# Weight parts issued behind the last eviction, and query weights behind the scores' low part

## The chip, the cores and the metric

One core of a Trainium2 chip runs one launch of the kernel. The metric is the device time of a launch in microseconds (us); a kernel is run three times and the median counts. The engines are named as in the profile: PE (TensorE), ACT (ScalarE), DVE (VectorE), POOL (GpSimd) and SP (SyncE, which here only starts transfers).

## The reference, cut to what matters

An encoder layer is applied to two requests, a prompt of 1024 tokens (A) and a sample of 512 (B), with the same weights. All numbers are 32-bit floats.

```python
h = rms_norm(x, pre_w)
cols = jnp.einsum('bsd,dc->bsc', h, w_in)
m_qk, m_v, m_o, m_z, m_i, m_f, a_qkv, a_z, gate = jnp.split(cols, ..., axis=-1)
y_m = mlstm_mixer(m_qk, m_v, m_o, m_i, m_f, ...) * silu(m_z)
y_a = dilated_attention(a_qkv, rel_table) * silu(a_z)
p_m = jnp.einsum('bsc,cd->bsd', y_m, w_pm)
p_a = jnp.einsum('bsc,cd->bsd', y_a, w_pa)
g = sigmoid(gate).reshape(b_, s_, 2, D_MODEL)
out = jnp.einsum('bsd,de->bse', g[:, :, 0] * p_m + g[:, :, 1] * p_a, w_out)
return x + rms_norm(out, post_w)
```

`mlstm_mixer` is a scan in chunks of 128 positions, in both directions, for four heads of 256 channels. In each chunk the scores q·k are weighted by an exponential of the gates (sc), num = sc·v + (wa·q)·C, and the state C is updated by C = decay·C + (ws·k)ᵀ·v. `dilated_attention` is a softmax over a window of keys, for three strides.

## The kernel before

A product of 32-bit floats is made of three matmuls (`mm3`, L209 to L211): each operand is split into a high part and a low part, and PE adds high·high, high·low and low·high. So everything that PE multiplies is first split: ACT copies the high part, and DVE or POOL subtracts it to get the low one.

*Order of work.* The prompt's projections fill the first 966 us. Then come the prompt's scan (64 rounds: 4 heads, 8 chunks, 2 directions; about 997 to 1310 us), the prompt's attention (to about 1635), the sample's scan (32 rounds; to about 1833), the sample's attention (to about 1957), and the merging of the branches with the last product. From 966 us on, "dense" units stand between the steps of scans and attention: products of 128 columns of a weight matrix with 512 tokens, for the sample's projections and later the branches. Each unit collects in one of two PSUM banks and is then emptied by an *eviction*: a function of its own for each kind of unit (`silu`, L746 and L749; `att_unit`, L772 and L774; the convolution's raw copy, L870; the gate's tanh, L896; `proj_m` and `proj_a`, L1643 and L1660; `close`, L1704 to L1711). PE can begin a unit only when the one before the last has been evicted.

*Weights.* `load_w` brings 512 KB into one of two raw buffers (`wraw`), by SP or, from the prompt's attention on, by POOL's queue. `split_w` (L263 to L283) issues the high part on ACT (L272) and the low part on DVE (L278) into a ring of pairs (`wh`/`wl`, later also `X0` and `Q1`). A raw buffer is free for the next load when the low part is done.

*Who sets the order.* PE's order and, from 966 us on, SP's are written by hand. Each other engine has one queue, worked off in order, whose order a scheduler picks at build time from its own estimates; `issue_after(x)` makes it put an instruction behind x. `split_w` already puts both parts behind `self.held` (the last four attention instructions on ACT or DVE), and the low part also behind `self.scans` (the scan's last DVE results).

*The scan.* `front(k)` prepares round k: POOL selects a mask (rm, L1103), ACT takes the exponential (L1105), DVE multiplies by the scores (L1106), ACT copies the high part (sch, L1109), POOL subtracts the low one (scl, L1110). From the second chunk on POOL also weights the queries with a row tile rw that a transfer brings (qw, L1114), ACT copies their high part (L1117), POOL subtracts the low one (ql, L1118). `core(k)` makes the products `num` and `kv` and updates the state: cf (L1149 for the first chunk, L1152 later), then its parts ch (L1176) and cl (L1177). There is one buffer for `kv`, so the next `kv` waits for cf.

*The attention.* For each tile of 128 queries: `products` (PE, lg), `softmax` (DVE adds the bias and takes the row maximum, L1374; nm, L1376; ACT takes exponentials, L1378), `turn` (PE transposes, L1385; a copy pts on ACT, L1388, or DVE, L1390) and `output` (PE o, L1398; ACT ot, L1400). The merged mLSTM rows ymr are split beside it (K0 on ACT, L1594; K1 on DVE, L1595).

Of the kernel before, what the change touches and what calls it, by code (L numbers as in the profile page):

```python
# [22 lines left out]
F32 = mybir.dt.float32  # L23
F32R = mybir.dt.float32r
AF = mybir.ActivationFunctionType
OP = mybir.AluOpType
# [3 lines left out]
P = 128  # L30
D = 1024
KT = D // P
BLK = 512
# [148 lines left out]
class Net:  # L182
    def __init__(self, tc, a):
        self.tc, self.nc, self.a = tc, tc.nc, a
        self.clock = self.lag = 0
        self.pending, self.owner = [], {}
        self.defer, self.mixed, self.rows = False, set(), {}
        self.queued, self.pace = [], 1
        self.side = self.nc.sync
        self.lows = None  # L190
        self.scans, self.state, self.held, self.sum = [], [], [], None
        self.low_part = None
        self.retired = []
        self.narrow, self.acc, self.direct = {}, [None, None], {}

# [68 lines left out]
    def split_w(self, raw, n):  # L264

        nc = self.nc
        hi, lo = self.wsplit.pop(0)
        self.wsplit.append((hi, lo))
        with ExitStack() as st:
            for x in self.held:  # L270
                st.enter_context(self.tc.issue_after(x.ins))
            high = nc.scalar.activation(hi[:, :n], raw[:, :n], AF.Copy)  # L272

        def rest():
            with ExitStack() as st:
                for x in (*self.held, *self.scans):
                    st.enter_context(self.tc.issue_after(x.ins))
                low = (self.lows or nc.vector).tensor_sub(lo[:, :n], raw[:, :n], hi[:, :n].bitcast(F32))  # L278
# [463 lines left out]
    def silu(self, c, g, w):  # L742

        nc = self.nc
        th = w()
        nc.scalar.activation(th, c, AF.Tanh, scale=0.5)  # L746
        if g is None:
            g = th
            nc.vector.scalar_tensor_tensor(g, th, 1.0, c, op0=OP.add, op1=OP.mult)  # L749
        else:  # L750
            nc.vector.scalar_tensor_tensor(g, th, 1.0, g, op0=OP.add, op1=OP.mult)
        return g
# [7 lines left out]
    def att_unit(self, j, c, T, w):  # L760

        nc, S = self.nc, T.S
        keys, g = j >= 12, j % 12 // 4
        dil = min(DILS[g], S // P)
        hi, lo = w(F32R), w(F32R)
        if g == 0 and not keys:
            parts = [(hi[:, :S - 64], lo[:, :S - 64], c[:, 64:]), (hi[:, S - 64:], lo[:, S - 64:], c[:, :64])]
        else:
            by = lambda z: z.rearrange("p (r i) -> p r i", r=dil)
            parts = [(by(hi), by(lo), c.rearrange("p (i r) -> p r i", r=dil))]  # L770
        for h, _, x in parts:
            nc.scalar.activation(h, x, AF.Copy, scale=1.0 if keys else 0.125)  # L772
        for h, l, x in parts:
            nc.vector.scalar_tensor_tensor(l, x, 1.0 if keys else 0.125, h.bitcast(F32), op0=OP.mult, op1=OP.subtract)  # L774
# [87 lines left out]
    def short_units(self, T):  # L862

        nc = self.nc
# [2 lines left out]

        def conv(u):
            def use(p):
                nc.scalar.activation(self.sraw[:, 1:1 + BLK], p, AF.Copy)  # L870
                self.conv_unit(u, T, self.sraw, w, False)
            return self.unit(u, use)

# [19 lines left out]
        def gate(br, ct):  # L893
            def use(p):
                t = w()
                nc.scalar.activation(t, p, AF.Tanh, scale=0.5)  # L896
# [139 lines left out]
    def mlstm(self, T, fill, steps, first, banks, lead, after, beside=()):  # L1036
# [10 lines left out]
        with ExitStack() as stack:  # L1047
# [45 lines left out]
            def front(k):  # L1093
# [13 lines left out]
                sch = sb.tile([P, P], F32R, name="sch")  # L1107
                scl = sb.tile([P, P], F32R, name="scl")
                nc.scalar.activation(sch, rm, AF.Copy)  # L1109
                nc.gpsimd.tensor_sub(scl, rm, sch.bitcast(F32))  # L1110
                m = made[k] = {"rw": rw, "sc": (sch, scl), "fl": flc}
                if i > 0:
                    qw = sb.tile([P, 2, P], F32, name="qw")
                    nc.gpsimd.tensor_tensor(qw, x["q"][:, :, cs], rw[:, 1][:, None, :].to_broadcast([P, 2, P]), op=OP.mult)  # L1114
# [502 lines left out]
    def branches(self, T, b, odd, before):  # L1617
# [12 lines left out]
        def proj_m(weights):  # L1630
            m2[:] = [self.place(1 - odd, i, F32) for i in (0, 2)]
            gate(1, 0)
            for ct in range(KT):
                wm = weights()
                pm = self.dense()
                for k in range(KT):
                    c = slice(k * P, (k + 1) * P)
                    hi, lo = yb[k // 4]
                    self.mm3(pm, (wm[0][:, c], wm[1][:, c]), (hi[:, k % 4], lo[:, k % 4]), k == 0, k == KT - 1)
                    if k == 3:  # L1640
                        gate(*((1, ct + 1) if ct < KT - 1 else (0, 0)))
                    if k == KT - 1:
                        nc.vector.scalar_tensor_tensor(m2[ct // 4][:, ct % 4], gates.pop((1, ct)), 1.0, pm, op0=OP.add, op1=OP.mult)  # L1643
                    yield

        def proj_a(weights):
            for ct in range(KT):
# [5 lines left out]
                for k in range(4):  # L1653
# [3 lines left out]
                        gate(0, ct + 1)  # L1657
                    if k == 3:
                        mg = self.osb.tile([P, BLK], F32, name="mg", bufs=2)
                        nc.vector.scalar_tensor_tensor(mg, gates.pop((0, ct)), 1.0, pa, op0=OP.add, op1=OP.mult)  # L1660
# [21 lines left out]
    def final(self, T, b):  # L1682
# [4 lines left out]
        def make(weights):  # L1687
# [13 lines left out]
            def close(u, t, c, p):  # L1701
                r0 = b * BLK + t * P
                o1 = sb.tile([P, BLK], F32, name="mg", bufs=2) if u else o[t]
                nc.scalar.activation(o1, p, AF.Square, accum_out=ss[:, t, u:u + 1])  # L1704
                if u == 0:
                    nc.vector.tensor_mul(o[t], p, pw[:, c])
# [4 lines left out]
                nc.vector.tensor_mul(o1, p, pw[:, c])  # L1711
# [339 lines left out]
```

## Time and profile before

| what | value |
|---|---|
| runs | 2256.8, 2258.14 and 2259.2 us, median 2258.14 |
| profiled execution | 2261.5 us, of which 1.8 outside the span |
| span, first to last instruction | 2259.7 us |
| busy: PE / DVE / ACT / POOL | 2244.2 / 1509.5 / 1129.2 / 718.6 us |
| granted TensorE clock | 1.000 |
| DMA | 418.27 MB, mean 185 GB/s |

A row of the timeline gives the start (from the span's start), the duration, the engine and line, what is written and read, and in brackets how long the engine had been idle and what ended that. A wait of PE counts in the end only because PE's order is fixed: whatever it waits for moves all that follows. An idle engine beside it costs nothing by itself.

### The profile page before, as it was taken

What the parts mean: (1) busy time and instruction counts of PE and PEld (TensorE: products, weight loads), DVE (VectorE), ACT (ScalarE), POOL (GpSimd) and SP (SyncE); (2) the same over time, 40 slices, a digit from 0 to 9 for tenths busy, and PEclk for the clock granted to TensorE, in tenths of its full rate; (3) what the DMA queues carried; (4) which work ended last, traced back from release to release, by engine and by line L of the source; (5) the groups of instructions that cost most, each with busy time, mean ns of one, the idle gap of its engine ahead of it and who ended that gap; (6) DMA issues with size and microseconds to landing.
All of it is one profiled execution on the core that took longest, in us unless ns stands there. A gap on an engine that the chain in (4) does not pass through costs nothing.

```text
span 2259.7 us, 35388 instructions
## 1 busy us (share of the span) xinstructions
PE 2244.2 (99%) x12226; PEld 1964.6 (87%) x12226; DVE 1509.5 (67%) x2875; ACT 1129.2 (50%) x2369; POOL 718.6 (32%) x1000
## 2 busy tenths in 40 slices
PE   9999999999999999999999999999999999999998
PEld 8999888888888888888888899999888888888887
DVE  7765577687776556558887755544689844655674
ACT  6432244344444434357777655566665644554332
POOL 1000333333333223237676610011165522221221
PEclk9999999999999999999999999999999999999999
DMA  3652455543332223284664789997678797776663
GB/s 123 168 134 76 172 205 192 192 176 121 112 111 103 84 84 140 103 298 153 226 223 127 191 217 235 253 245 221 203 248 284 238 278 211 233 251 200 233 230 109
DMA packets 222685, 418.27 MB, mean 185 GB/s; under 512 B 24841, under 2 KB 128969, under 8 KB 222506
## 3 DMA queue, kind: packets, MB, share of 16 engines
q1 hardware_dynamic: 194536, 315.86, 44.4%
q0 software_dynamic: 24368, 87.56, 12.4%
q10 hardware_dynamic: 3602, 12.59, 1.4%
q8 instruction: 97, 1.59, 0.3%
q14 instruction: 82, 0.67, 0.1%
HBM read 296.19 MB, written 128.12 MB: 188 GB/s over the span
## 4 chain that ended last, share of the span: by engine, by line
PE 95%; DMA 2%; issue 1%; ACT 1%; POOL 1%; DVE 0%; DVEq 0%; SPq 0%; POOLq 0%; ACTq 0%
PE d L211 14%; PE d L209 14%; PE d L210 14%; PE dense L209 12%; PE dense L211 12%; PE dense L210 12%; PE o L1398 4%; PE pt L1385 2%; PE lg L1362 2%; PE num L211 1%; PE num L209 1%; PE num L210 1%; PE kv L209 1%; PE a L1070 1%; PE kv L210 1%
## 5 line engine op out<-in xcount | busy, mean ns | idle before, releaser
L209 PE MATMUL dense<-H,wh 128*128 128x512 f32 x664 | 270.6, 408 | 0.8 <-DVE V0b L1643 0.8
L211 PE MATMUL dense<-H,wl 128*128 128x512 f32 x664 | 260.9, 393 | 0.0
L210 PE MATMUL dense<-H,wh 128*128 128x512 f32 x664 | 260.2, 392 | 0.0
L210 PE MATMUL d<-Hl,phla 128*128 128x512 f32 x608 | 236.5, 389 | 0.0
L211 PE MATMUL d<-Hh,phla 128*128 128x512 f32 x608 | 236.5, 389 | 0.0
L209 PE MATMUL d<-Hh,phla 128*128 128x512 f32 x608 | 236.5, 389 | 0.0
L278 DVE TENSOR_TENSOR wl<-wraw,wh 128x1024 fp32r<-128x1024 f32 (+1 forms) x121 | 149.3, 1234 | 70.0 <-ACT wh L272 69.9
L1374 DVE CUSTOM_DVE_ANT_0 ls<-lg,bias 128x256 f32<-128x256 f32 (+1 forms) x288 | 93.7, 362 | 132.8 <-PE lg L1362 71.2
L211 PE MATMUL d<-Hh,phlb 128*128 128x512 f32 x456 | 177.4, 389 | 0.0
L209 PE MATMUL d<-Hh,phlb 128*128 128x512 f32 x456 | 177.4, 389 | 0.0
L210 PE MATMUL d<-Hl,phlb 128*128 128x512 f32 x456 | 177.4, 389 | 0.0
L687 POOL TENSOR_TENSOR psum_w<-pw_raw 128x512 f32<-128x512 f32 x38 | 58.0, 1527 | 365.1 <-DMA pw_raw<-w_in 208.8
L1378 ACT ACTIVATE ls<-ls,nm 128x256 f32<-128x256 f32 (+1 forms) x288 | 130.3, 454 | 84.0 <-DVE nm L1376 59.2
L272 ACT ACTIVATE wh<-wraw 128x1024 fp32r<-128x1024 f32 (+1 forms) x124 | 128.7, 1038 | 77.1 <-PE dense L210 27.0
L211 PEld LDWEIGHTS dense<-H,wl 128*128 128x128 f32 x664 | 124.6, 188 | 28.2
L209 PE MATMUL d<-vhi,Hh 128*128 128x322 f32 x448 | 140.9, 315 | 0.3
L211 PE MATMUL d<-vhi,Hl 128*128 128x322 f32 x448 | 140.3, 313 | 0.4 <-DVE Hl L396 0.2
L210 PE MATMUL d<-vlo,Hh 128*128 128x322 f32 x448 | 139.7, 312 | 0.0
L209 PEld LDWEIGHTS dense<-H,wh 128*128 128x128 f32 x664 | 125.0, 188 | 15.5 <-DVE V0b L1643 1.2
L210 PEld LDWEIGHTS dense<-H,wh 128*128 128x128 f32 x664 | 125.4, 189 | 14.3
L211 PEld LDWEIGHTS d<-Hh,phla 128*128 128x128 f32 x608 | 114.1, 188 | 23.7
L210 PEld LDWEIGHTS d<-Hl,phla 128*128 128x128 f32 x608 | 114.2, 188 | 23.6
(570 smaller groups left out, 6166.4 us busy)
## 6 DMA issues: line engine op xcount, KB each, us to landing
pw_raw<-w_in SPq DMA_DIRECT2D x76, 512.0 KB
wraw<-w_in SPq DMA_DIRECT2D x64, 512.0 KB
aqk_a<-pwk SPq DMA_DIRECT2D x48, 512.0 KB
aqk_b<-sw SPq DMA_DIRECT2D x48, 256.0 KB
wraw<-w_pm POOLq DMA_DIRECT2D x24, 512.0 KB, 6.1
wraw<-w_out POOLq DMA_DIRECT2D x24, 512.0 KB, 4.0
wraw<-w_v POOLq DMA_DIRECT2D x22, 430.0 KB, 7.3
erep<-erow SPq DMA_DIRECT2D x16, 512.0 KB
```

The lines of the kernel that those rows point to most:

```text
L209: nc.tensor.matmul(out, lh, rh, start=start, stop=False)
L210: nc.tensor.matmul(out, lh, rl, start=False, stop=False)
L211: nc.tensor.matmul(out, ll, rh, start=False, stop=stop)
L272: high = nc.scalar.activation(hi[:, :n], raw[:, :n], AF.Copy)
L278: low = (self.lows or nc.vector).tensor_sub(lo[:, :n], raw[:, :n], hi[:, :n].bitcast(F32))
L687: self.nc.gpsimd.tensor_add(s[:, 0], ws[1][:, 0], ws[1][:, 1])
L1070: nc.tensor.matmul(p[:, c - c0], kT[:, ct, c * P:(c + 1) * P], qT[:, ct, c * P:(c + 1) * P], start=ct == 0, stop=ct == 1)
L1362: nc.tensor.matmul(lg[:, hh, c:c + w], q[hh][:, qs], z[:, k0:k0 + w], start=z is k[hh], stop=z is not k[hh])
L1374: nc.vector.tensor_tensor_reduce(out=ls[:, hh], in0=ts["lg"][hh], in1=bt[:, hh], scale=1.0, scalar=NEG, op0=OP.add, op1=OP.max, accum_out= ...
L1378: self.held = self.held[-3:] + [nc.scalar.activation(ls[:, hh], ls[:, hh], AF.Exp, bias=nm[:, hh:hh + 1], accum_out=ot[:, 128 + hh:129 + hh])]
L1385: nc.tensor.transpose(pp[:, hh * nk + x], ts["ls"][:, hh, x * P:(x + 1) * P], self.ident)
L1398: nc.tensor.matmul(po[:, hh * 64:hh * 64 + 64], pt[:, hh * nk + x], v[:, kt[x], c0 + hh * 64:c0 + hh * 64 + 64], start=x == 0, stop=x == n ...
```

## The change

Two edits. First, each eviction notes its instructions in `self.evicted`, and `split_w` puts the high part and the low part of a weight behind those of the last eviction, besides `self.held`. Second, in the first eight rounds of each scan the weighting of the queries on POOL is put behind the low part of the scores of the same round. Nothing is added or taken away; PE's order and SP's stay as they are.

```diff
         self.scans, self.state, self.held, self.sum = [], [], [], None
-        self.low_part = None
+        self.low_part, self.evicted = None, []
...
         with ExitStack() as st:
-            for x in self.held:
+            for x in (*self.held, *self.evicted):
                 st.enter_context(self.tc.issue_after(x.ins))
             high = nc.scalar.activation(hi[:, :n], raw[:, :n], AF.Copy)
 
         def rest():
             with ExitStack() as st:
-                for x in (*self.held, *self.scans):
+                for x in (*self.held, *self.evicted, *self.scans):
                     st.enter_context(self.tc.issue_after(x.ins))
...
-        nc.scalar.activation(th, c, AF.Tanh, scale=0.5)
+        self.evicted = [nc.scalar.activation(th, c, AF.Tanh, scale=0.5)]
         if g is None:
             g = th
-            nc.vector.scalar_tensor_tensor(g, th, 1.0, c, op0=OP.add, op1=OP.mult)
+            self.evicted.append(nc.vector.scalar_tensor_tensor(g, th, 1.0, c, op0=OP.add, op1=OP.mult))
...
-                nc.scalar.activation(t, p, AF.Tanh, scale=0.5)
+                self.evicted = [nc.scalar.activation(t, p, AF.Tanh, scale=0.5)]
...
                 nc.scalar.activation(sch, rm, AF.Copy)
-                nc.gpsimd.tensor_sub(scl, rm, sch.bitcast(F32))
+                low = nc.gpsimd.tensor_sub(scl, rm, sch.bitcast(F32))
...
-                    nc.gpsimd.tensor_tensor(qw, x["q"][:, :, cs], rw[:, 1][:, None, :].to_broadcast([P, 2, P]), op=OP.mult)
+                    with self.tc.issue_after(low.ins) if k < 8 else ExitStack():
+                        nc.gpsimd.tensor_tensor(qw, x["q"][:, :, cs], rw[:, 1][:, None, :].to_broadcast([P, 2, P]), op=OP.mult)
```

The evictions of `att_unit`, the convolution, `proj_m`, `proj_a` and `close` are noted in the same way. Because of added lines, a line of before from L774 on is one higher in the changed kernel, two from L1114 and three from L1644.

Three places show how rows move. The first is POOL at the start of the prompt's scan (about 982 to 1003 us); rm, scl, qw and ql carry a number for their round, rw0 to rw3 are row tiles. Before:

```order
L1103 AFFINE_SELECT rm_8069<-rw0_7902 128x128
L1114 TENSOR_TENSOR qw_8146<-Q0_7883,rw0_7902 128x256
L1103 AFFINE_SELECT rm_8085<-rw1_7903 128x128
L1114 TENSOR_TENSOR qw_8213<-Q0_7883,rw1_7903 128x256
L1110 TENSOR_TENSOR scl_8076<-rm_8069,sch_8075 128x128
L1103 AFFINE_SELECT rm_8136<-rw0_7902 128x128
L1118 TENSOR_TENSOR ql_8149<-qw_8146,qh_8148 128x256
L1118 TENSOR_TENSOR ql_8216<-qw_8213,qh_8215 128x256
L1114 TENSOR_TENSOR qw_8275<-Q0_7883,rw2_7904 128x256
L1110 TENSOR_TENSOR scl_8092<-rm_8085,sch_8091 128x128
L1110 TENSOR_TENSOR scl_8143<-rm_8136,sch_8142 128x128
L1103 AFFINE_SELECT rm_8203<-rw1_7903 128x128
```

In the changed kernel POOL's rows at the same place are:

```order
L1111 TENSOR_TENSOR scl_8092<-rm_8085,sch_8091 128x128
L1111 TENSOR_TENSOR scl_8143<-rm_8136,sch_8142 128x128
L1116 TENSOR_TENSOR qw_8146<-Q0_7883,rw0_7902 128x256
L1104 AFFINE_SELECT rm_8203<-rw1_7903 128x128
L1104 AFFINE_SELECT rm_8265<-rw2_7904 128x128
L1120 TENSOR_TENSOR ql_8149<-qw_8146,qh_8148 128x256
L1111 TENSOR_TENSOR scl_8210<-rm_8203,sch_8209 128x128
L1116 TENSOR_TENSOR qw_8213<-Q0_7883,rw1_7903 128x256
L1104 AFFINE_SELECT rm_8337<-rw3_7905 128x128
L1120 TENSOR_TENSOR ql_8216<-qw_8213,qh_8215 128x256
L1111 TENSOR_TENSOR scl_8272<-rm_8265,sch_8271 128x128
L1116 TENSOR_TENSOR qw_8275<-Q0_7883,rw2_7904 128x256
```

scl_8092 and scl_8143 now stand ahead of all qw, and qw_8275, which waits for row tile rw2, stands behind them; ql_8216 now stands behind the select of rw3.

The second place is ACT at the start of the sample's attention (about 1839 to 1851 us); sw0 and sw1 are evictions of gate units, wh1 is the high part of a weight. Before:

```order
L272 ACTIVATE Q1_18766<-wraw1_7754 128x1024
L272 ACTIVATE wh1_7757<-wraw0_7753 128x1024
L896 ACTIVATE sw0_7871<-dense_18811 128x512
L1378 ACTIVATE ls_18906,ot1_18786<-ls_18906,nm_18907 128x256 x2
L1594 ACTIVATE K0_18817<-ymr0_18770 128x512
L1378 ACTIVATE ls_18955,ot2_18787<-ls_18955,nm_18956 128x256 x2
L896 ACTIVATE sw1_7872<-dense_18879 128x512
```

In the changed kernel ACT has there:

```order
L272 ACTIVATE Q1_18766<-wraw1_7754 128x1024
L897 ACTIVATE sw0_7871<-dense_18811 128x512
L1380 ACTIVATE ls_18906,ot1_18786<-ls_18906,nm_18907 128x256 x2
L1596 ACTIVATE K0_18817<-ymr0_18770 128x512
L1380 ACTIVATE ls_18955,ot2_18787<-ls_18955,nm_18956 128x256 x2
L272 ACTIVATE wh1_7757<-wraw0_7753 128x1024
L897 ACTIVATE sw1_7872<-dense_18879 128x512
```

wh1 moved from ahead of the eviction sw0 to behind the exponentials of ls_18955, just ahead of the next eviction.

The third place is DVE right behind it (about 1846 to 1863 us); wl1, wl2, wl0 and X0 are low parts of weights, ls the softmax tiles. Before:

```order
L278 TENSOR_TENSOR wl1_7758<-wraw0_7753,wh1_7757 128x1024
...
L1390 COPY pts_18917<-pt_18784 128x512
...
L278 TENSOR_TENSOR wl2_7760<-wraw1_7754,wh2_7759 128x1024
L1374 ISA ls_19001,ot3_18788<-lg_18946,bias1_18796 128x256
...
L1376 TENSOR_SCALAR nm_19002<-ot3_18788 128x2
L278 TENSOR_TENSOR wl0_7756<-wraw0_7753,wh0_7755 128x1024
L1374 ISA ls_19061,ot4_18789<-lg_18996,bias2_18797 128x256
...
L1390 COPY pts_19013<-pt_19008 128x512
L278 TENSOR_TENSOR X0_18765<-wraw1_7754,X0_18765 128x1024
L1376 TENSOR_SCALAR nm_19062<-ot4_18789 128x2
```

In the changed kernel DVE has there:

```order
L1392 COPY pts_18917<-pt_18784 128x512
...
L278 TENSOR_TENSOR wl1_7758<-wraw0_7753,wh1_7757 128x1024
L278 TENSOR_TENSOR wl2_7760<-wraw1_7754,wh2_7759 128x1024
L278 TENSOR_TENSOR wl0_7756<-wraw0_7753,wh0_7755 128x1024
L1376 ISA ls_19001,ot3_18788<-lg_18946,bias1_18796 128x256
...
L1376 ISA ls_19061,ot4_18789<-lg_18996,bias2_18797 128x256
...
L1392 COPY pts_19013<-pt_19008 128x512
L1378 TENSOR_SCALAR nm_19002<-ot3_18788 128x2
L1378 TENSOR_SCALAR nm_19062<-ot4_18789 128x2
L278 TENSOR_TENSOR X0_18765<-wraw1_7754,X0_18765 128x1024
```

The three low parts wl1, wl2 and wl0 now stand together ahead of the reductions of ls_19001, which stood ahead of wl0.

More of the change, by code (lines that the diff above doesn't have):

```diff
@@ L771, in att_unit @@
         for h, _, x in parts:
-            nc.scalar.activation(h, x, AF.Copy, scale=1.0 if keys else 0.125)
+            self.evicted = [nc.scalar.activation(h, x, AF.Copy, scale=1.0 if keys else 0.125)]
         for h, l, x in parts:
-            nc.vector.scalar_tensor_tensor(l, x, 1.0 if keys else 0.125, h.bitcast(F32), op0=OP.mult, op1=OP.subtract)
+            low = nc.vector.scalar_tensor_tensor(l, x, 1.0 if keys else 0.125, h.bitcast(F32), op0=OP.mult, op1=OP.subtract)
+        self.evicted.append(low)
         self.put(("aqk", T.S, j), T.aqk[0, j], hi.bitcast(F32), hi)
@@ L869, in use @@
             def use(p):
-                nc.scalar.activation(self.sraw[:, 1:1 + BLK], p, AF.Copy)
+                self.evicted = [nc.scalar.activation(self.sraw[:, 1:1 + BLK], p, AF.Copy)]
                 self.conv_unit(u, T, self.sraw, w, False)
@@ L1642, in proj_m @@
                     if k == KT - 1:
-                        nc.vector.scalar_tensor_tensor(m2[ct // 4][:, ct % 4], gates.pop((1, ct)), 1.0, pm, op0=OP.add, op1=OP.mult)
+                        self.evicted = [nc.vector.scalar_tensor_tensor(m2[ct // 4][:, ct % 4], gates.pop((1, ct)), 1.0, pm,
+                                                                       op0=OP.add, op1=OP.mult)]
                     yield
```

8 lines of the change are left out of this document (4 added, 4 removed).

## The prediction

> **What bounds the kernel now.** I read the page first, then the list of what each engine waited for, then the timeline around each wait.
>
> ```profile
> span 2259.7 us, 35388 instructions
> ...
> PE 2244.2 (99%) x12226; PEld 1964.6 (87%) x12226; DVE 1509.5 (67%) x2875; ACT 1129.2 (50%) x2369; POOL 718.6 (32%) x1000
> ...
> PE 95%; DMA 2%; issue 1%; ACT 1%; POOL 1%; DVE 0%; DVEq 0%; SPq 0%; POOLq 0%; ACTq 0%
> ```
>
> TensorE (PE) is busy for 2244.2 of 2259.7 us and holds 95% of the chain that ended last. Its order is written out by hand and both programs have the same one. So the change can only take away, or add, moments in which PE waits. The list of PE's waits says how many there are; the columns are the sum, the count and the longest, in us:
>
> ```profile
> PE num L211 <- POOL scl L1110: 1.2, 1, 1.2
> PE kv L209 <- DVE cf L1152: 1.2, 2, 0.6
> ...
> PE dense L209 <- DVE V0b L1643: 0.8, 1, 0.8
> PE dense L209 <- ACT sw L896: 0.7, 1, 0.7
> ...
> PE kv L209 <- DVE r L1163: 0.4, 1, 0.4
> PE o L1398 <- ACT pts L1388: 0.2, 1, 0.2
> PE num L209 <- DVE X L1169: 0.2, 1, 0.2
> ...
> PE kv L209 <- DVE cf L1149: 0.2, 1, 0.2
> ```
>
> These rows, with the left-out ones of the start, are all waits of PE that the profile shows. They sum to 4.9 us and all lie behind 990 us, where the reordering begins. A first matmul behind a wait also runs 0.1 us longer (0.50 for 0.39 us in the fourth place below), about 1 us for the nine. **The ceiling of any gain is 6 us**, 0.26%. A measurement of this kernel can tell about 0.2%, or 4.5 us, from no change.
>
> **The change part by part.** No instruction, transfer or byte is added or removed; only rows of ACT, DVE and POOL change places, all between 974 and 1873 us. So each term is one place where PE waits now, or where a moved row may make it wait.
>
> *First place, the start of the prompt's scan.* Timeline of POOL, ACT and PE; the columns are start, duration, engine, line, names, and in brackets the idle time with what ended it:
>
> ```profile
> 997.10 1.19 POOL L1114 TENSOR_TENSOR qw<-Q,rw 128x256 f32<-128x256 f32 x1 [1.68 <-DMA rw<-rw_a]
> 998.25 0.86 POOL L1110 TENSOR_TENSOR scl<-rm,sch 128x128 fp32r<-128x128 f32 x2
> ...
> 994.92 0.31 ACT L1109 ACTIVATE sch<-rm 128x128 fp32r<-128x128 f32 x1 [0.20 <-DVE rm L1106]
> ...
> 998.76 0.39 PE L211 MATMUL num<-V0a,scl 128*128 128x258 f32 x1 [1.17 <-POOL scl L1110]
> ```
>
> POOL stood in qw, which waited for a row tile to land, and the two scl behind it came at 998.25, though the high parts that they need were there by 995.23 (994.92 + 0.31). In the new order both scl stand ahead of every qw. They can run from 995.2, and PE, which has waited since 997.59 (998.76 less 1.17), finds the first of them done even if it takes the longest time of the row at the end of the next fence, 1.44. **Gain 1.2.** The weighting then comes later: qw and ql of rounds 2 and 3 run between 996 and 1003.5, since one select among them waits for the row tile that ended POOL's idling at 1002.31.
>
> ```profile
> 1002.31 1.40 POOL L1114 TENSOR_TENSOR qw<-Q,rw 128x256 f32<-128x256 f32 x1 [2.69 <-DMA rw<-rw_a]
> ...
> 1005.87 0.28 PE L211 MATMUL num<-ch,ql 128*128 128x258 f32 x1
> ...
> 1011.12 0.28 PE L211 MATMUL num<-ch,ql 128*128 128x258 f32 x1
> ...
> L1110 POOL TENSOR_TENSOR scl<-rm,sch x96: 448/468/1439, 984.7 to 1798.2; 128x128 fp32r<-128x128 f32 x96
> ```
>
> PE uses them at 1005.87 and 1011.12, so 7 us cover the move; its cost is 0. If that cover were gone, each us late would cost one. The same edit in the sample's scan moves rows that no wait of PE names: 0.
>
> The last row gives the least, median and longest time of a scl in ns.
>
> *Second place, the end of the same scan, where DVE has no room.* Timeline of ACT, DVE, POOL and PE:
>
> ```profile
> 1278.52 1.05 ACT L272 ACTIVATE wh<-wraw 128x1024 fp32r<-128x1024 f32 x1
> 1279.48 0.57 ACT L746 ACTIVATE sg<-dense 128x512 f32<-128x512 f32 x1
> ...
> 1280.08 0.69 DVE L749 SCALAR_TENSOR_TENSOR sg<-sg,dense 128x512 f32<-128x512 f32 x1 [0.61 <-ACT sg L746]
> ...
> 1281.08 1.58 DVE L278 TENSOR_TENSOR wl<-wraw,wh 128x1024 fp32r<-128x1024 f32 x1
> ...
> 1287.67 0.74 DVE L1152 SCALAR_TENSOR_TENSOR cf<-cf,rw,kv 128x516 f32<-128x516 f32 x1
> 1288.97 0.69 DVE L751 SCALAR_TENSOR_TENSOR sg<-sw,sg 128x512 f32<-128x512 f32 x1 [0.56 <-ACT sw L746]
> ...
> 1281.56 1.42 POOL L1110 TENSOR_TENSOR scl<-rm,sch 128x128 fp32r<-128x128 f32 x1
> ...
> 1284.34 0.36 PE L209 MATMUL kv<-V1a,kh 128*128 128x258 f32 x1 [0.64 <-DVE cf L1152]
> ...
> 1289.23 0.28 PE L209 MATMUL kv<-V1a,kh 128*128 128x258 f32 x1
> ```
>
> Now the weight's high part runs before the eviction sg, DVE idles 0.61 us for that eviction, and everything behind it up to the state update cf is late. With the eviction first, DVE starts 0.5 us or so sooner and the 0.64 wait at 1284.34 nearly goes. But at 1287.67 the new order puts the second eviction (0.69) ahead of cf, which had 0.82 to spare (1289.23 less 1288.41). Moved behind it, cf ends about 0.7 later, and PE comes about 0.5 sooner: up to 0.5 comes back there. The waits near 1277 and 1295 (0.2 and 0.4) may shrink with DVE's idle time. Bounds: 0 to the 1.2 of the three waits. I take the middle, **gain 0.6**. The wait at 1745 keeps its DVE rows ahead of it and stays.
>
> The weight's subtraction took 1.58 us here, beside a scl of 1.42 on POOL, where its like take 1.22 (fourth place) and the median scl 0.47: each seems to hold up the other. [...]
>
> *Third place, the start of the sample's attention.* ACT and PE:
>
> ```profile
> 1844.84 1.06 ACT L272 ACTIVATE wh<-wraw 128x1024 fp32r<-128x1024 f32 x1 [4.68 <-DMA wraw<-w_pm]
> 1845.80 0.58 ACT L896 ACTIVATE sw<-dense 128x512 f32<-128x512 f32 x1
> ...
> 1846.43 0.50 PE L209 MATMUL dense<-H,X 128*128 128x512 f32 x1 [0.72 <-ACT sw L896]
> ```
>
> A high part that waits 4.68 us for its load holds up the eviction behind it, and PE waits for the bank. The new order has the eviction ahead; its unit ended a whole unit of PE's work earlier, since the two banks take turns, so the wait goes. **Gain 0.7.** What is late next is the weight itself, which now stands behind more rows.
>
> *Fourth place, 14 us later, where the change adds a wait.* The weight part wl0 waits for a load, and in the new order the softmax reductions of ls_19001 (L1374) stand behind it instead of ahead:
>
> ```profile
> 1852.38 0.42 DVE L1374 CUSTOM_DVE_ANT_0 ls<-lg,bias 128x256 f32<-128x256 f32 x1
> ...
> 1853.18 0.17 DVE L1376 TENSOR_SCALAR nm<-ot 128x2 f32<-128x2 f32 x1
> 1853.92 1.22 DVE L278 TENSOR_TENSOR wl<-wraw,wh 128x1024 fp32r<-128x1024 f32 x1 [0.56 <-ACT wh L272]
> ...
> 1855.74 0.69 DVE L1390 COPY pts<-pt 128x512 f32<-128x512 f32 x1
> ...
> 1853.79 0.49 ACT L1378 ACTIVATE ls<-ls,nm 128x256 f32<-128x256 f32 x1
> ...
> 1834.69 0.53 POOL L261 DMA_DIRECT2D wraw<-w_pm  x1 [1.78 <-DVE X L278]
> ...
> 1860.66 0.60 PE L1385 MATMUL pt<-ident,ls 128*128 128x128 f32 x4
> ...
> wraw<-w_pm POOLq DMA_DIRECT2D x24, 512.0 KB, 6.1
> ...
> DMA to landing us min/median/max: 5.3/7.7/10.1
> ```
>
> The last two rows give the time from issue to landing: the page's median of these 24 loads, and least, median and longest of the five that POOL issues from 1834 to 1860. Here the chain, each step with its own row's time. The low part X0 of that buffer moves behind two reductions, a subtraction and a small row (0.42 to 0.7 each now), so the load of 1834.69 goes out at about 1836.2. It lands 10.1 later, as now (1844.84 less 1834.69), at 1846.3; high part (1.06) to 1847.4, low part (1.22) to 1848.6, next load out at 1848.9. With the median of 6.1 this lands at 1855.0; high part to 1856.1, low part to 1857.3. Then two reductions and a small row (0.97 now, from 1852.38 to 1853.35), two reductions and a copy (1.29 now, from the end of wl at 1855.14 to 1856.43): 1859.6. Two exponentials of 0.49 end at 1860.6. PE turns that tile at 1860.66, or 1859.9 once the third place's 0.7 is gone. **Loss 0.8**, by bounds of 0 (a load of 5.3) and 4.8 (one of 10.1). I take 6.1 because this very load is the shortest of the five now and will meet the same transfers, but later.
>
> Sum: 1.2 + 0.6 + 0.7 - 0.8 = 1.7 us less. From the profiled execution's 2261.5 (span and 1.8 around it) that gives 2259.8; this execution lies 3.4 above the median of the runs, 2258.14, so the forecast is **2256.4**.
>
> **The rivals.** *Full gain:* the load at the fourth place takes 5.3, and all of the second place's 1.2 goes: 3.1 less, 2255.0. For it: that load takes 5.3 now; against: DVE's lack of room around 1288. Chance 0.18. *Low parts hold up the softmax (the slower side):* every row of DVE behind wl0 waits with it. It decides from a second load of 7.8 us on: there the wait, 2.5, eats all three gains. At 10.1 it is 4.8, and the sum is 2260.4; a second tile late by the same costs 4.8 more, 2265.2. For it: the 10.1 of the first load. Against: behind 1873 us no row moves, so it can hit two or three tiles only. Chance 0.17, a third of it over 2262.7. *Weighting late or GpSimd blocked at the first place:* by times near the longest of the scl row, or by a late row tile, the 1.2 comes back as a wait for ql or scl: 2257.6. Chance 0.08. *The change does not do what it says* is excluded for the order; the rows moved. Something that no row shows: 0.05, mostly slower.
>
> **How the numbers follow.** My forecast has 0.52. Faster by over 0.2% means under 2253.6, which needs 4.5 of the ceiling's 6: 0.04. Slower by over 0.2%, over 2262.7: 0.06 from the slower rival and 0.04 from the unknown, 0.10. The rest, 0.86, is within. The range goes from 2253.8 (3.1 and the spread of the runs, 1.2 to a side) to 2261.0 (the slower rival with one tile late, and 0.7 of that spread).
>
> **What would show it.** Right: the list of PE's waits loses "num <- scl" and "dense <- sw"; kv waits near 1284 shrink; a wait of pt for ACT's ls of 0 to 2.4 us appears near 1859. Wrong: waits of num for ql near 1006, of kv for cf that grow in count, or several of pt or o between 1855 and 1875.

## The result, and the profile after

The change made the kernel slower: 2265.35 us median (2263.6 to 2267.2), against 2258.45 for the kernel before on the same chip; the ratio is 1.0028, with a 95% interval of 1.0021 to 1.0035. The prediction, 2256.4 in a range to 2261.0, was wrong in size and in sign. The profiled execution of the changed kernel took 2264.7 us (span 2262.6), that of before 2261.5, so the two profiles differ by 3.2 of the 6.9 us: before's lies 3 above its own median.

The page of the changed kernel, in the lines that answer to those of before: PE works 1.0 us longer and holds a point less of the chain, DVE a point or two more.

```profile
span 2262.6 us, 35332 instructions
...
PE 2245.2 (99%) x12226; PEld 1966.9 (87%) x12226; DVE 1505.1 (67%) x2875; ACT 1125.5 (50%) x2369; POOL 718.8 (32%) x1000
...
PE 94%; DMA 2%; DVE 2%; issue 1%; ACT 1%; POOL 0%; DVEq 0%; POOLq 0%; ACTq 0%
```

Its list of PE's waits (sum, count, longest in us):

```profile
PE lg L1364 <- DVE ot L1376: 3.3, 1, 3.3
...
PE dense L209 <- ACT sw L897: 1.9, 1, 1.9
PE pt L1387 <- ACT ls L1380: 0.8, 1, 0.8
...
PE num L209 <- ACT X L1169: 0.7, 1, 0.7
```

All that the prediction named is gone: num for scl, the three between 1277 and 1295 (one of num, two of kv), dense for sw at 1846, dense for V0b at 2026. In their place stand two long ones. Where they lie is best seen on one instruction of each tile, the scores lg of the sample's attention. First the kernel before, then the changed one:

```profile
1832.71 0.64 PE L1362 MATMUL lg<-V0a,Q 128*128 128x256 f32 x4
...
1841.88 0.64 PE L1362 MATMUL lg<-V0a,Q 128*128 128x256 f32 x4
...
1854.16 0.72 PE L1362 MATMUL lg<-V1a,Q 128*128 128x256 f32 x4
1860.10 0.72 PE L1362 MATMUL lg<-V1a,Q 128*128 128x256 f32 x4
1866.06 0.72 PE L1362 MATMUL lg<-V1a,Q 128*128 128x256 f32 x4
```

```profile
1828.19 0.64 PE L1364 MATMUL lg<-V0a,Q 128*128 128x256 f32 x4
...
1839.54 0.64 PE L1364 MATMUL lg<-V0a,Q 128*128 128x256 f32 x4
...
1850.80 0.72 PE L1364 MATMUL lg<-V1a,Q 128*128 128x256 f32 x4
...
1855.93 1.00 PE L1400 MATMUL o<-X,pts 128*128 128x64 f32 x8
1860.24 1.20 PE L1364 MATMUL lg<-V1a,Q 128*128 128x256 f32 x4 [3.31 <-DVE ot L1376]
1862.21 1.18 PE L1387 MATMUL pt<-ident,ls 128*128 128x128 f32 x4 [0.77 <-ACT ls L1380]
...
1869.49 0.73 PE L1364 MATMUL lg<-V1a,Q 128*128 128x256 f32 x4
```

The changed kernel comes to the sample's attention 4.5 us ahead (1832.71 less 1828.19). The wait of dense at 1836 takes that to 2.3, the prediction's third place gives back 1.0 (3.4 ahead at 1850.80), and then it loses 6.8 within two tiles: 18.69 us from 1850.80 to 1869.49, where the kernel before needs 11.90. Two waits, 3.31 and 0.77, make 4.1 of that. The rest is TensorE's clock. Stretches of the changed kernel; the columns are the busy times of PE, its weight loads, DVE, ACT and POOL (with counts), then the granted clock, the share of the DMA and GB/s:

```profile
1858.00:1860.00 2.00, 0.00 (x0) 0.00 (x0) 1.82 (x4) 0.80 (x3) 0.30 (x1) 0.81 0.38 143
1860.00:1862.00 2.00, 1.20 (x4) 0.93 (x4) 1.53 (x9) 0.45 (x2) 0.23 (x1) 0.50 0.85 202
...
1866.00:1868.00 2.00, 2.00 (x10) 1.59 (x10) 1.99 (x3) 2.00 (x8) 1.96 (x5) 0.98 0.84 307
```

From 1859.3 to 1866.1 the clock is 0.50, and the dense matmuls begin 0.43 us apart there, behind it 0.23. PE is busy for 5.09 us of that; by the clock I estimate that half of it, 2.5 us, is lost beside the waits. 4.1 and 2.5 make 6.6 of the 6.8. The two are not independent: lg takes 1.20 us in place of 0.72, and pt behind it, which waits for ACT, would have waited that 0.5 longer at full clock. By itself the clock costs about 2.0, an estimate from these rows.

Why does lg wait? ACT, DVE and POOL of the changed kernel, followed back from it:

```profile
1836.53 1.05 ACT L272 ACTIVATE X<-wraw 128x1024 fp32r<-128x1024 f32 x1
...
1846.14 0.51 ACT L1380 ACTIVATE ls<-ls,nm 128x256 f32<-128x256 f32 x1 [2.12 <-DVE nm L1378]
...
1847.14 1.04 ACT L272 ACTIVATE wh<-wraw 128x1024 fp32r<-128x1024 f32 x1
...
1857.09 1.06 ACT L272 ACTIVATE wh<-wraw 128x1024 fp32r<-128x1024 f32 x1 [5.86 <-DMA wraw<-w_pm]
...
1858.18 1.23 DVE L278 TENSOR_TENSOR wl<-wraw,wh 128x1024 fp32r<-128x1024 f32 x1 [6.17 <-ACT wh L272]
1859.32 0.42 DVE L1376 CUSTOM_DVE_ANT_0 ls<-lg,bias 128x256 f32<-128x256 f32 x1
```

```profile
1835.51 0.63 ACT L1596 ACTIVATE K<-ymr 128x512 fp32r<-128x512 f32 x1 [6.38 <-DMA ymr<-ym_a]
```

```profile
1839.13 0.53 POOL L261 DMA_DIRECT2D wraw<-w_pm  x1 [1.42 <-DVE X L278]
...
1849.74 0.53 POOL L261 DMA_DIRECT2D wraw<-w_pm  x1 [4.16 <-DVE wl L278]
```

In order of time: the split K0 of a row tile (an earlier one than the K0_18817 shown under *The change*, which runs at 1843.39) stands on ACT ahead of the eviction sw3 and of X0's high part, and waits 6.38 us for its load. X0's low part, which frees the raw buffer, is late with it, and the load goes out at 1839.13 in place of the 1836.2 that I had worked out for a later PE. It lands 5.9 us later, at 1845.06, but its high part wh1 stands on ACT behind the exponentials of ls_18955 and begins only at 1847.14. The next load goes out at 1849.74 and lands at 1857.0; the low part wl0 follows at 1858.18, and the reductions of ls_19001 stand behind it until 1859.32, though their scores were made two lg before. The lg of 1860.24 needs the bank that they read.

My theory after this was that the loss is made at the sample's attention, by reductions that queue on DVE behind a low part, with the half clock on top. The rivals were that the loads are too slow in any order, that waits differ from execution to execution, and that PE's own lead makes the wait. Each expectation says what its letters stand for.

### The profile page after: what moved, and what is told of

The parts are those of the page before. It is cut to its first block, busy times and chain, and to the rows that moved or that the text cites. A ratio compares the mean times of both kernels' runs of the same rounds, so it can differ in the third digit from the quotient of the medians.

```text
span 2262.6 us, 35332 instructions
## 1 busy us (share of the span) xinstructions
PE 2245.2 (99%) x12226; PEld 1966.9 (87%) x12226; DVE 1505.1 (67%) x2875; ACT 1125.5 (50%) x2369; POOL 718.8 (32%) x1000
## 3 DMA queue, kind: packets, MB, share of 16 engines
q8 instruction: 97, 1.59, 0.3%
## 4 chain that ended last, share of the span: by engine, by line
PE 94%; DMA 2%; DVE 2%; issue 1%; ACT 1%; POOL 0%; DVEq 0%; POOLq 0%; ACTq 0%
PE d L211 14%; PE d L209 14%; PE d L210 14%; PE dense L209 12%; PE dense L211 12%; PE dense L210 12%; PE o L1400 4%; PE pt L1387 2%; PE lg L1364 2%; PE num L209 1%; PE num L211 1%; PE num L210 1%; PE a L1071 1%; DMA ymr<-ym_a 1%; PE kv L210 1%
```

## The experiments

All times are medians; the kernel before was measured beside each set of runs at 2257.9 to 2258.45.

*Each edit alone.* The first edit alone puts `with ExitStack():` back at qw:

```diff
-                    with self.tc.issue_after(low.ins) if k < 8 else ExitStack():
+                    with ExitStack():
```

> The change without its second edit: only the weights' parts behind the evictions. Theory Q (queue): the loss is made in the sample's attention, where a split of ymr that waits for a load stands ahead of an eviction on ACT, and reductions stand behind a weight part that waits for a load on DVE; these loads, not PE, set when the waits end. So giving the 1.2 us of the first scan's start back only shortens the later waits: 2264 to 2266, PE's wait of lg near 1860 about 2 instead of 3.3 us, and the half clock behind it stays. Theory L (late start): the two edits add up independently: 1.3 us slower than the change, 2266.7, with the wait of lg unchanged at 3.3.

Measured: 2266.43, ratio 1.0031 (1.0020 to 1.0043). The whole loss comes from this edit. Its profile has the wait of lg (2.6, shorter, as Q has it), that of pt (1.3) and slow matmuls behind them (the dense ones begin 0.43 us apart, later 0.23), but the time is nearer L's 2266.7; it doesn't tell the two theories apart.

The second edit alone takes `self.evicted` out of both lists of `split_w`:

```diff
-            for x in (*self.held, *self.evicted):
+            for x in self.held:
...
-                for x in (*self.held, *self.evicted, *self.scans):
+                for x in (*self.held, *self.scans):
```

> Only the second edit: query weights behind the scores' low part. Theory Q: PE's wait of num for scl at 998 goes and nothing replaces it in the sample's attention, since its order is that of before: 1 to 1.3 us less than before, 2257.2. Theory E (any earlier PE runs into the transfers of the sample's attention and gives the time back there): same as before within 0.3 us, 2258.4, with a longer wait of dense for sw near 1845.

Measured: 2257.15, ratio 0.9992 (0.9984 to 1.0001): 1.2 us less, as expected and the size of the prediction's first place, though the interval reaches no change. Of the three waits between 1277 and 1295 its profile has one left (0.39).

*Evictions noted for part of the time.* A flag `note` switches the first edit on and off; each kernel sets it at other places:

```diff
-            for x in (*self.held, *self.evicted):
+            for x in (*self.held, *(self.evicted if self.note else ())):
...
-                for x in (*self.held, *self.evicted, *self.scans):
+                for x in (*self.held, *(self.evicted if self.note else ()), *self.scans):
```

Off from the sample's attention on:

> Both edits, but the parts go behind evictions only until the sample's attention begins; there the reductions stand ahead of wl0 again, and X0's high part ahead of the ymr split, while the eviction sw3 still stands behind that split. Theory Q: no wait of lg near 1860 and no half clock; a wait of dense for sw of 1 to 2 us near 1836 and one of 0.7 near 1843 stay: 4.4 earlier up to there, so 2256 to 2257. Theory E: the 4.4 us come back as waits in the sample's attention: 2258 or more.

Measured: 2259.8, ratio 1.0004 (0.9996 to 1.0013). lg doesn't wait, the clock stays at 1.00, and 5.5 us of the loss are gone; but the time is E's and not Q's. Off from the sample's scan on:

> Both edits, but the parts go behind evictions only until the sample's scan begins; from there on the order is that of before. Theory Q: 3 us gained up to 1640 us, all else as before (waits of kv near 1745 and 1777, of dense near 1846): 2255.5. Theory E: 2258 or more, the 3 us coming back as longer waits behind 1830.

Measured: 2258.54, ratio 0.9997 (0.9988 to 1.0006). Again E's side: the parts ahead don't bring the 3 us that the profiles seemed to promise. On only from the middle of the prompt's scan (`k == 31`) to the end of the prompt's attention:

> Both edits, but the evictions are noted only from the middle of the prompt's scan (round 32 of 64) to the end of the prompt's attention: without the new waits near 1078 and 1096 us, and without the sample's scan and attention. Theory Q (the change is worth what its gains at the end of the scan and in the prompt's attention are, 1.3 for the weighting and 1.5 to 2.5 for the evictions): 2258.4 - 1.3 - 2.0 = 2255.1. Rival V (the waits of the kernel before at 1277 to 1295 and 1475 differ from execution to execution and were only long in its profile, so the evictions are worth nothing there): 2257.1, the same as the weighting alone.

Measured: 2255.57, ratio 0.9988 (0.9979 to 0.9997), the fastest kernel of all, and the only one whose interval lies wholly below 1. Q's side; but what the evictions add to the weighting alone, some 1.3, isn't clear of the noise, since the two intervals overlap. PE doesn't wait between 1270 and 1300 in its profile. On only up to the middle of the prompt's scan:

> Both edits, but evictions noted only up to the middle of the prompt's scan (round 32 of 64). Theory Q (the early half costs what the run with late notes lacks against the run with notes up to the sample's scan, 2258.5 - 2255.6 = 3.0): 2257.15 + 3.0 = 2260.1, with waits near 1078, 1082 and 1096 us that the weighting alone doesn't have. Rival V (these two runs differ for other reasons, the waits there are 0.7 us each at most): 2257.2 to 2258.

Measured: 2258.55, ratio 1.0003 (0.9994 to 1.0011), 1.4 more than the weighting alone, between the two expectations. The first half of that scan costs something: in its profile num waits 0.69 for ACT's X at 1096 and kv 0.39 for cf at 1077. The 3.0 between the two runs before it isn't explained by this alone.

*The second profile of the kernel before.*

> The kernel before, once more, for a second profile. Theory V (its short waits for loads and for ACT and DVE behind them differ from execution to execution): the wait of 1.2 for scl at 998 is there again, since it comes from the order on POOL; the waits at 1277 to 1295, 1745, 1846 and 2026 are there in part, with other lengths, and the profiled time lies within 2256 to 2262. Rival F: the same list of waits within 0.1 us each.

```profile
PE num L211 <- POOL scl L1110: 0.9, 1, 0.9
...
PE kv L209 <- DVE cf L1152: 0.6, 1, 0.6
...
PE dense L209 <- ACT sw L896: 0.2, 1, 0.2
```

2259.21 us. Theory V holds: scl is there again (0.9 for 1.2), one kv wait of 0.6 in place of two, sw 0.2 in place of 0.7, V0b none in place of 0.8; only the kv waits for cf of L1149 grew, from 0.2 to 0.5. Of the 6 us that I called the ceiling, some 2 were this one execution's.

*The queue and the clock at the fourth place.* One instruction, wl0, on POOL in place of DVE:

```diff
+        self.nth += 1
+        low_on = nc.gpsimd if self.nth == 5 else self.lows or nc.vector
...
-                low = (self.lows or nc.vector).tensor_sub(lo[:, :n], raw[:, :n], hi[:, :n].bitcast(F32))
+                low = low_on.tensor_sub(lo[:, :n], raw[:, :n], hi[:, :n].bitcast(F32))
...
+            N.nth = 0
             N.attend(B, fill, STEPS[3], kept["qkv"], ("lg", "o", "pt"), 7)
```

> The changed kernel, but one instruction, the low part wl0 behind which the reductions of ls_19001 stand, is made by POOL in place of DVE (2.4 us there in place of 1.2). Theory Q (the wait is DVE's queue: reductions that have been ready for long stand behind a subtraction that waits for a load): the wait of lg for ot (3.3) goes; the exponentials still stand behind the weight's high part on ACT, so pt waits 1.5 to 2 in place of 0.8, and a dense matmul perhaps 0.5 for wl0; if these waits are too short to halve the clock, 2265.35 - 3.3 - 2.7 + 1.0 + 0.5 = 2260.9, if it is halved all the same 2263.5. Rival L (the load itself is what PE pays for, whoever queues behind it): the wait turns up at the dense matmuls that use that weight, 2265 or more.

Measured: 2261.16, ratio 1.0014 (1.0005 to 1.0023): some 4 us come back from one moved subtraction. Its ACT, POOL and PE:

```profile
1855.55 1.06 ACT L274 ACTIVATE wh<-wraw 128x1024 fp32r<-128x1024 f32 x1 [5.65 <-DMA wraw<-w_pm]
...
1856.75 2.35 POOL L280 TENSOR_TENSOR wl<-wraw,wh 128x1024 fp32r<-128x1024 f32 x1 [4.07 <-ACT wh L274]
...
1855.51 0.72 PE L1366 MATMUL lg<-V1a,Q 128*128 128x256 f32 x4
1857.80 1.17 PE L1389 MATMUL pt<-ident,ls 128*128 128x128 f32 x4 [1.57 <-ACT ls L1382]
```

The weight is as late as ever, and lg doesn't wait. Q holds against L; what is left is the exponentials behind the high part on ACT, as expected, 1.57. Behind that wait the clock is 0.50 from 1858.3 to 1861.7.

The product o of the second tile made four times, so that PE works during the wait:

```diff
-                for hh in range(2):
+                for hh in [0, 1] * times:
...
-        return [stages(i % 2, *x) for i, x in enumerate(tiles)]
+        return [stages(i % 2, *x, times=4 if n <= 4 and u == 0 and i == 1 else 1) for i, x in enumerate(tiles)]
```

> The changed kernel, but the product o of the sample's second tile, which stands just ahead of the lg that waits 3.3 us, is made four times in place of once into the same bank (three repeats of 0.85 us; the result is the same). PE then works for 2.6 of the 3.3 us of that wait; the moment at which lg can start stays the same. Theory C (the half granted clock behind the wait is the price of PE standing idle): the clock stays at 1.00, the dense matmuls behind lg take 0.39 us again, and half of the 5.6 us at half clock comes back: 2265.35 - 2.7 = 2262.6. Rival N (the half clock has nothing to do with the idle time): clock still 0.50 for some 5.6 us, 2265.3; if the repeats push lg back, more.

> The kernel with o made four times, once more, for a profile of an execution that isn't its fastest. Theory C: where the lg that follows still waits, it waits 2.6 us less than in the changed kernel, and the clock stays at 1.00. Rival N: the clock falls to 0.50 near 1860 to 1866 all the same, 2265.

Measured: 2265.2, ratio 1.0029 (1.0020 to 1.0039); the two profiled executions took 2261.3 and 2263.2. The second of them, PE and its stretches:

```profile
1855.03 3.68 PE L1400 MATMUL o<-X,pts 128*128 128x64 f32 x32
1859.51 0.71 PE L1364 MATMUL lg<-V1a,Q 128*128 128x256 f32 x4 [0.80 <-DVE ot L1376]
1861.48 0.93 PE L1387 MATMUL pt<-ident,ls 128*128 128x128 f32 x4 [1.26 <-ACT ls L1380]
...
1860.00:1862.00 2.00, 0.69 (x5) 0.25 (x4) 0.81 (x5) 1.17 (x5) 0.00 (x0) 1.00 0.84 217
```

lg can start as late as in the changed kernel (4.48 us after that o began, there 4.31), but the clock stays at 1.00. In the other profile lg doesn't wait, and the clock is 1.00 too. So at this lg the half clock went with PE's idling, 3.31 us in the changed kernel against 0.80 and none. The mean granted clocks of all executions agree: the changed kernel's fifteen have 0.997 or 0.998, seven of these ten 0.999 or 1.000, the values of the kernel before. But the median, which theory C put at 2262.6, doesn't move, and that of the seven alone is 2265.2 too. The clock mostly comes back and the time doesn't; why stays open.

*A row's high part on DVE*, so that ACT's queue doesn't stand behind it (the scheduler then also puts the reductions ahead of wl0):

```diff
+                    if T.n > 4 and (b, row, j, k) == (0, 0, 1, 2):
+                        nc.vector.tensor_copy(hi[:, k - 2, :w], t[:, :w])
+                    else:
+                        nc.scalar.activation(hi[:, k - 2, :w], t[:, :w], AF.Copy)
```

> The changed kernel, but one row's high part, K0 from ymr0 at the start of the sample's attention, is copied by DVE in place of ACT, so ACT's eviction sw3 and the weight's high part X0 don't stand behind that row's load. By itself this takes away the dense wait of 1.9 us and lets X0, and with it the load of the next weight, go some 1 us earlier; the scheduler, with its other estimates, also puts the reductions of ls_19001 ahead of wl0 again. Theory Q (both losses are rows that queue behind a part that waits for a load): waits dense<-sw and lg<-ot both go, and with them the half clock: 2265.35 - 1.9 - 3.3 - 0.8 - 2.7 = 2256.7, up to 2258.5 if pt still waits for exponentials behind the high part wh0. Rival L (loads are too slow for PE here, so PE has to wait for one of them in any order): only part comes back, 2262 to 2263.5.

Measured: 2260.8, ratio 1.0008 (0.9999 to 1.0017): some 4 of 6.9 us come back, between the two expectations. Two things changed at once here, so the run doesn't tell which of them did it. In its profiled execution (2257.25) PE doesn't wait once in the sample's attention, so the median's other 2 to 3 us aren't seen in the trace.

*Which stretches does the loss need?* Evictions noted only from the sample's attention on, without the second edit:

> The kernel before with the first edit alone, and evictions noted only in the sample's attention and behind it; some eight rows of ACT and of DVE change places, among them X0's high part behind an eviction, wh1 behind two exponentials, and wl0 ahead of the reductions of ls_19001; nothing ahead of 1830 us changes. Theory Q (the loss is made here, by rows that push the chain of loads back and put the softmax behind it): 2258.4 + 5.5 = 2263.9, with a wait of lg for ot and the half clock near 1860. Rival P (the loss needs PE to come early, since the loads keep their own pace; the change's PE is there some 3 us earlier): the wait is 0 to 1, without half clock, 2258 to 2260.

Measured: 2258.58, ratio 1.0002 (0.9993 to 1.0011). Theory Q as I had it falls: wl0 stands ahead of the reductions as in the changed kernel, and nothing is lost. The order on ACT is not the changed kernel's, though: X0's high part stands ahead of K0 here, and wh1 (1843.36) ahead of the exponentials of ls_18955 (1844.32). Its ACT, POOL, DVE and PE:

```profile
1831.92 1.05 ACT L272 ACTIVATE X<-wraw 128x1024 fp32r<-128x1024 f32 x1
1832.87 0.62 ACT L1596 ACTIVATE K<-ymr 128x512 fp32r<-128x512 f32 x1
...
1834.53 0.53 POOL L261 DMA_DIRECT2D wraw<-w_pm  x1 [3.37 <-DVE X L278]
...
1853.22 1.23 DVE L278 TENSOR_TENSOR wl<-wraw,wh 128x1024 fp32r<-128x1024 f32 x1 [2.83 <-ACT wh L272]
1854.36 0.42 DVE L1376 CUSTOM_DVE_ANT_0 ls<-lg,bias 128x256 f32<-128x256 f32 x1
...
1857.60 0.72 PE L1364 MATMUL lg<-V1a,Q 128*128 128x256 f32 x4
```

K0 doesn't wait, and the load goes out 23.1 us ahead of the lg that could wait (1857.60 less 1834.53); in the changed kernel it was 17.8 to the moment at which PE was ready (1860.24 less 3.31, less 1839.13). The first two reductions begin at 1854.36, 3.2 us before that lg. So a second cause is needed. Two theories were left: the order at the end of the sample's scan, which makes K0 wait (J), or PE's lead from the gains ahead (P). Notes from the sample's scan on, nothing ahead of it and no second edit:

> The first edit alone, with evictions noted only from the sample's scan on; nothing before 1635 us changes, so PE comes to the sample's attention no earlier than in the kernel before. Theory J (two stretches make the loss together: the sample's scan's end puts weights and rows back so that the row K0 waits some 6 us for its load on ACT with the eviction and X0's high part behind it, and the sample's attention has its reductions behind the low part whose load goes out late for that): 2258.2 + 6.3 = 2264.5, with K0 waiting 4 to 7 us, the load after X0 out 17.7 us ahead of the end of that o, a wait of lg for ot of 2 to 4 and the half clock. Rival P (the loss needs a PE that has gained 3 us by then): 2258.5 to 2260, a wait of lg under 1.

Measured: 2266.23, ratio 1.0034 (1.0021 to 1.0047): the whole loss. In its profile PE isn't early at the tile ahead of the wait (lg at 1854.87; 1854.16 and 1852.64 in the two profiles of the kernel before). J's parts are there, not all in J's sizes: K0 waits 7.1, the load goes out 19.3 us before PE is ready for lg, which waits 1.5 and not 2 to 4, and a wait of dense of 2.1, ended at 1839.24, has about 3.4 us of half clock of its own, from 1839.1. Both edits everywhere except the first half of the prompt's scan and the sample's scan:

> Both edits, evictions noted from the middle of the prompt's scan to the end of the prompt's attention and again from the sample's attention on; only the first half of the prompt's scan and the sample's scan are left as before. PE comes early here, but K0 doesn't wait. Theory J: no loss at the sample's attention, and the wait of dense for sw (1.9 in the profile with notes to the prompt's attention) may go: 2254 to 2255.6. Rival P: lg waits 2 to 4 again, 2258.5 to 2262.

Measured: 2256.1, ratio 0.9994 (0.9985 to 1.0003): the early PE (lg at 1849.38, in the changed kernel 1850.80), and no loss. Both runs answer for J and against P. The row K0 of the first of them, on ACT, and of the run without notes in the sample's attention (2259.8):

```profile
1838.07 0.63 ACT L1596 ACTIVATE K<-ymr 128x512 fp32r<-128x512 f32 x1 [7.12 <-DMA ymr<-ym_a]
...
1839.08 1.05 ACT L272 ACTIVATE X<-wraw 128x1024 fp32r<-128x1024 f32 x1
```

```profile
1831.38 1.05 ACT L272 ACTIVATE X<-wraw 128x1024 fp32r<-128x1024 f32 x1
1837.13 0.63 ACT L1596 ACTIVATE K<-ymr 128x512 fp32r<-128x512 f32 x1 [4.69 <-DMA ymr<-ym_a]
```

With the sample's scan noted K0 waits 4.4 to 7.1 us in every one of these profiles; without it, 0.3 at most. Where the sample's attention isn't noted, X0 stands ahead of that wait and only one eviction is late (dense waits 1.14); where both are and ACT splits K0, X0 stands behind it, and the chain of loads starts late. Where only the attention is noted, X0 stands ahead of K0, which doesn't wait. So two stretches are shown to make the loss together; no run tells K0's wait from the order on ACT that comes with it. Neither stretch costs much alone (1.4 with all that is ahead of it, and 0.7), together they cost 8.3.

## Why the prediction was wrong, point by point

- *First place, gain 1.2: right.* The wait, 0.8 to 1.2 in the five profiles without this edit, is gone, and the weighting alone measured 1.2 less. Nothing waits for ql near 1006.
- *Second place, gain 0.6: the mechanism fits, the size stays unsure.* Two or all of the three waits from 1277 to 1295 stand in all four profiles without either edit there. They are gone in that of the first edit alone, all 1.2 and not half; but the second edit alone leaves only 0.39 of them too, so they aren't the notes' doing alone. The wait at 1745, of which I said that it stays, went, as it did in the second profile of the kernel before. But the same edit brought a wait of num for ACT's X at 1096 (0.7), which I didn't look for: I had priced the places where PE waited before, and none where a moved row makes a new wait in the first half of that scan.
- *The ceiling of 6 us: too high.* It came from one execution that lay 3 us above its median, and the second profile shows that 2 us of its waits come and go. It also counted the 0.8 of V0b, which lay at 2026, behind the last row that moves.
- *Third place, gain 0.7: right for that profile* (the second profile of the kernel before has 0.2 there), with an eviction earlier in the same stretch that I missed. Further up ACT's queue, sw3 and X0 had come to stand behind K0; that costs 1.9 at 1836.
- *Fourth place, loss 0.8 by bounds of 0 and 4.8: the step that failed.* The loss was the end of a chain of loads (1860.6) less PE's arrival (1859.9), and both moments were off. The chain began with "so the load of 1834.69 goes out at about 1836.2". I had followed X0's low part on DVE, where it moved behind two reductions, a subtraction and a small row, and had left its high part where it was. That one had moved too, behind K0 on ACT, and K0 waits for a transfer that the order of the sample's scan delays. The load went out at 1839.13. It took 5.9 us where I had kept 10.1, so it landed ahead of my 1846.3; but I had let wh1 begin when its load lands, and it stood behind the exponentials of ls_18955. So the next load went out at 1849.74 for my 1848.9, took 7.3 for my 6.1 (within my 5.3 to 10.1), and pt began at 1862.21, 1.6 behind my 1860.6. PE's arrival was off by more. I had taken only the third place's 0.7 off, as if the chain moved along with all that PE gains further ahead. It didn't: the rows of V0b were loaded from 1820.30 on, before from 1820.04, while PE was ready for this lg at 1856.93, before at 1860.10. With the 0.56 from lg to pt of one tile before, it could have turned the tile at about 1857.5, not 1859.9. The wait showed first at lg, which needs the bank that the reductions read, and not at pt alone. In all PE waited 4.1 and not 0.8.
- *The upper bound of that term, 4.8,* also left out the half clock that came with the wait, 2.5 us by the estimate above, which the sum put at nothing. The whole term measured 6.8.
- *The slower rival* had the right mechanism with 0.17, "every row of DVE behind wl0 waits with it", but its condition was a second load of 7.8 us or more. It decided at 7.3, because the chain ran late and PE came early. The range ended at 2261.0 since I gave that rival one late tile and no clock. That its 2265.2, for a load of 10.1 and two late tiles, lies beside the measured 2265.35 is chance.
- *"The change does not do what it says"* was rightly excluded: the rows moved as they should. They were the wrong rows to move at two of the four stretches.

One cause further back stays open: why a row's load takes longer when the sample's scan is noted. The load that K0 waits for and its split, first in the kernel before, then POOL's row in the changed kernel:

```profile
1825.89 0.54 POOL L250 DMA_DIRECT2D ymr<-ym_a  x1 [3.19 <-DVE V1b L1595]
...
1833.52 1.27 ACT L1594 ACTIVATE K<-ymr 128x512 fp32r<-128x512 f32 x2
```

```profile
1827.95 0.54 POOL L250 DMA_DIRECT2D ymr<-ym_a  x1 [5.01 <-DVE V1b L1597]
```

It goes out 2.1 us later, in a kernel whose PE is 4.5 earlier, since the row V0b ahead of it took 6.0 us to land where it took 4.2 before. And it takes 7.5 itself, before 5.8. Weights' loads go out close to rows' in both kernels, and no run separated them.

## What to carry to other kernels

When a change reorders one operation that has two halves on two engines, follow both halves: the half that isn't in the row you look at may have moved behind a wait of its own. Where work is released by a chain of loads, price the moment at which the chain starts against the moment at which the bottleneck engine arrives, not only the length of one load; two reorderings that are harmless alone can each use up the same slack. Take a second profile of the kernel before, if there is one, before waits of half a microsecond are counted as a gain.

## What the runs showed of the hardware that I had not expected

The granted clock fell to 0.50 around short waits of TensorE. It was 0.50 for 6.8 us in the changed kernel (1859.3 to 1866.1) and for 3.4 us with wl0 on POOL (1858.3 to 1861.7). The run with notes from the sample's scan on has two such stretches, about 3.4 us from 1839.1 and 6.8 from 1863.0, an estimate from its mean clocks (0.78 in 1838 to 1840, 0.75 in 1862 to 1864, 0.54 in 1868 to 1870) and the lengths of its matmuls. In the profile of the first edit alone the dense matmuls begin 0.43 us apart from 1865.1 to 1869.4, and 0.23 behind that. The row of the stretch with wl0 on POOL:

```profile
1858.30:1861.70 3.40, 3.40 (x9) 2.78 (x10) 1.74 (x4) 2.83 (x7) 1.58 (x3) 0.50 0.69 191
```

The wait ahead of this stretch was one of 1.57 us. The length of the wait alone doesn't decide: one of 2.1 (notes from the sample's scan on) had half clock with it, but with waits of 1.59 (o made four times, second profile) and 1.91 (notes from the middle of the prompt's scan to its attention) the clock stayed at 1.00, and so it did with the 1.88 that ended at 1836.68 in the changed kernel:

```profile
1836.00:1838.00 2.00, 1.32 (x6) 1.10 (x7) 1.16 (x3) 2.00 (x5) 0.54 (x1) 1.00 1.08 235
```

What else decides, no run shows.
